# Turning x later and moving gate projections between groups in a hand-ordered state space stage

## The chip, the cores and the metric

One Trainium2 chip, one of its cores. The metric is the device time of one execution in microseconds (us), where less is better. Everything is float32 at the kernel's edges.

## What is computed

Two layers of a hybrid encoder on one sequence of 512 tokens and 1024 channels. In each layer one input projection feeds a state space branch (Mamba-2 style, forward and backward), a differential attention branch and a cross-attention branch; the branches are merged by gates computed from x. What matters here is the state space branch and the gates:

```python
proj = jnp.einsum('bsd,de->bse', x, w_in[layer])
z, xbc, dt_raw, dq, dk, dv, dg, cq, cg, gl = jnp.split(proj, splits, axis=-1)
# _ssd_branch: 32 heads of 64 channels, 4 groups of 8 heads, state 128, chunks of 128 tokens
xbc = jax.nn.silu(_centred_dwconv(xbc, conv_w, conv_b))      # 5 taps; x 2048, B 512, C 512 channels
y_diag = jnp.einsum('bcqgn,bcsgn,bgrcqs,bcsgrp->bcqgrp', cm, bm, decay, xs)
states = jnp.einsum('bcqgn,bgrcq,bcqgrp->bcgrpn', bm, decay_states, xs)
# scan over the 4 chunks: h -> h * chunk_decay + states; prev = the h before each chunk
y_off  = jnp.einsum('bcqgn,bcgrpn,bgrcq->bcqgrp', cm, prev, jnp.exp(a_cum))
y = (y_fwd + y_bwd + d_skip * xs) * jax.nn.silu(z);  y = _rmsnorm(y, norm_w)
...
merged = gates[:, :, 0] * (y_ssd @ w_br_ssd) + gates[:, :, 1] * (y_diff @ w_br_diff) + gates[:, :, 2] * (y_cross @ w_br_cross)
```

## The kernel before

Channels lie on the partitions and the 512 tokens along the free axis. A float32 matrix product is made from three matmuls on a high and a low part (`xh`, `xl` of the input; `wh`, `wl` of a weight; `mm3`). The work is a list of **units**. A unit is 128x1024 floats of weights (`wr`, 512 KB, loaded by SP at line 134), which ACT rounds to `wh` (line 87) and DVE subtracts to `wl` (line 77), and then 24 matmuls of 128x512 on TensorE (PE, line 99) into one bank of PSUM (`pj`, three buffers). A unit can be cut in the middle, and other matmuls put there.

The state space stage `ssd()` takes the four groups one after another in each layer. For a group g the units are: `bu` and `cu` (B and C), `xu(g, 0..3)` (x, 128 channels each, block b), `zu(g, 0..3)` (the gate z) and, for the group before, `wu(p, 0..3)` with p = g-1 (that branch's output projection: 24 matmuls for each of its two 128-channel outputs over half of a unit, copied or added into `mrg`). Twelve units are **early gates** (`gu`): gate projections that are not needed here and fill the stage; each ends in a Tanh on ACT (`tg`) and a store by SP. Between units stand small pieces of PE work:

- `bturn`, `xturn(g, b)`: four 128x128 transposes of the convolved, SiLU'd B or x block (`bC`, `xsC`) into the bank `pt` (one buffer); ACT copies it to `bT` or to a quarter of `xsT`. The convolution of an x unit is one scaled copy on ACT and four taps on DVE (`acc`, line 80), then SiLU on ACT.
- `states(g, 0..2)`: DVE multiplies `xsT` by the decays to `xw` (two buffers), and PE forms two state matrices of the chunk; ACT or DVE turns them into `prev`.
- `expos(g, b)`, no PE work: for each of the block's two heads SP loads a row of cumulative sums, broadcast to 128 partitions, into `ab` (two buffers, 512 KB, line 551); DVE takes the minimum with a mask, ACT makes eight exponentials of 128x128 in place, DVE adds the two directions and multiplies by `gs` into `m` (three buffers). The next load into the same `ab` buffer can be issued when that `m` is done.
- `block(g, b)`: 6 matmuls with `prev`, 16 with `m` (22 of 128x128 in all, more rows in the trace), then on DVE and ACT the output `y`, split into `yh` and `yl` for `wu`.

ACT needs another function table for the exponentials than for SiLU and Tanh: an `ACT_TABLE_LOAD` stands at each change between them.

**What sets the order.** PE's order in this stage is written out by hand: `U(unit, pieces...)` places a unit with pieces in its middle, `J(piece)` a piece between units, and the stage runs under `self.tc.manual_schedule(engines={mybir.EngineType.PE})`. The orders of ACT, DVE and SP are made by the Tile scheduler when the kernel is built. Each engine works its own list off in order.

Of the kernel before, what the change touches and what calls it, by code (L numbers as in the profile page):

```python
# [51 lines left out]
class Net:  # L52
# [391 lines left out]
    def ssd(self, l):  # L444
# [54 lines left out]
        def xpart(g, b):  # L499
            def f(wh, wl):  # L500
                x = yield from self.proj2(wh, wl)
                xc = B["xsC", g, b] = self.t(self.sp, [P, S], f"xsC{b}")
                self.conv(x, 4 * g + b, xc)
            return f
# [28 lines left out]
        def zpart(g, b):  # L533
            def f(wh, wl):
                ps = yield from self.proj2(wh, wl)
                sz = B["sz", g, b] = self.t(self.sp, [P, S], "sz", bufs=2)
                self.act(sz, ps, AF.Silu)
            return f
# [57 lines left out]
        def wpart(g, u):  # L596
            def f(wh, wl):
                yh, yl = G["y", g]
                pss = [self.bank(self.pj, "pj") for _ in range(2)]

                ks = ((0, 1, 2), (3,)) if u == 0 else ((0, 1, 2, 3),)
                for n, kk in enumerate(ks):
                    for i, ps in enumerate(pss):
                        for k in kk:
                            c = slice(k * 256 + i * P, k * 256 + (i + 1) * P)
                            self.mm(ps, wl[:, c], yh[:, k, :], k == 0, False)
                            self.mm(ps, wh[:, c], yh[:, k, :], False, False)
                            self.mm(ps, wh[:, c], yl[:, k, :], False, k == 3)
                        if 3 in kk:
                            o = self.br[:, 2 * u + i, :]  # L610
                            if g == 0:
                                self.act(o, ps)
                            else:
                                self.tt(o, o, ps, ALU.add)
                        if n == i == 0:
                            yield
            return f
# [63 lines left out]
        def U(unit, *amid):  # L681
            gen, u = unit

            def f(wh, wl):
                g = gen(wh, wl)
                next(g, None)
                for fn, *args in amid:
                    fn(*args)
                next(g, None)
            self.T(f, u)  # L690

        def J(fn, *args):
            self.T(lambda: fn(*args))

        def bu(g):
            return bpart(g), (l, UB + g)

        def cu(g):
            return cpart(g), (l, UC + g)

        def xu(g, b):
            return xpart(g, b), (l, UXS + 4 * g + b)

        def zu(g, b):
            return zpart(g, b), (l, UZ + 4 * g + b)

        def wu(g, u):
            return wpart(g, u), (l, UBS + 4 * g + u)

        def gu():  # L710
            return early.pop(0)
# [36 lines left out]
        for g in range(1, 4):  # L748
            p = g - 1
            U(bu(g))  # L750
            if g == 1:
                J(states, 0, 2)
                U(zu(p, 1), (block, p, 0))
            else:
                J(block, p, 0)
                U(zu(p, 1))
            J(expos, p, 1)
            U(cu(g))
            U(gu())
            J(block, p, 1)  # L760
            U(xu(g, 0), (bturn, g))
            J(expos, p, 2)
            U(zu(p, 2), (within, g))
            U(xu(g, 1))
            J(block, p, 2)
            J(xturn, g, 0)
            U(zu(p, 3))
            J(expos, p, 3)
            U(xu(g, 2))
            J(xturn, g, 1)  # L770
            J(block, p, 3)
            U(xu(g, 3))
            U(gu(), (xturn, g, 2))
            U(wu(p, 0))
            J(xturn, g, 3)
            U(wu(p, 1))
            U(wu(p, 2), (states, g, 0))
            J(states, g, 1)
            U(wu(p, 3))
            J(states, g, 2)  # L780
            J(expos, g, 0)
            U(zu(g, 0))
# [648 lines left out]
```

## Time and profile before

| what | value |
|---|---|
| device time, median of 3 runs | 2189.69 us (2188.62 to 2190.12) |
| the profiled execution: its time | 2190.09 us |
| the profiled execution: its span | 2188.3 us |
| PE busy | 2148.1 us, 98% |
| DVE busy, ACT busy | 71%, 53% |
| mean granted TensorE clock | 0.997 of full |
| state space stage of layer 0, of layer 1 | about 80 to 500 us, about 1150 to 1640 us |

The span is the time from the first to the last instruction in the profiled execution; the 1.8 us around it belong to the execution's own time. Busy times are sums over the span. A row of the timeline has the start in us, the duration, engine, line, operation and tiles, and, where the engine stood idle just before, in brackets the idle time and what ended it.

### The profile page before, as it was taken

Reading aid. Unit: us, or ns where it says so; the run is one execution under the profiler, and the core shown is the slowest. Engines: PE = TensorE matmul, PEld = TensorE weight load, DVE = VectorE, ACT = ScalarE, POOL = GpSimd, SP = SyncE. Lnnn points to the kernel's source line nnn. Section 1 sums busy time; section 2 is a strip of 40 time slices with the busy share of each in tenths; the row PEclk is TensorE's granted clock in tenths of the full one; section 3 lists DMA queues with packets and bytes.
Section 4 is the critical chain, followed back from the end, with each engine's and each line's share of the span. In section 5 each row is a group of like instructions: output and inputs, shape, how many; then the busy total and the mean of one; then the engine's idle time right before and its main releaser. Section 6 shows DMA issues by size and latency. Waiting matters only on the chain.

```text
span 2188.3 us, 29240 instructions
## 1 busy us (share of the span) xinstructions
PE 2148.1 (98%) x11122; PEld 1787.3 (82%) x11122; DVE 1546.6 (71%) x2404; ACT 1152.1 (53%) x2035; POOL 61.3 (3%) x38
## 2 busy tenths in 40 slices
PE   8999999999999999999999999999999999999998
PEld 6787878788888888887888777878788888888876
DVE  5677777869554788766566677878675547888667
ACT  5676757554432455543345676858533325555430
POOL 0010101010000000000000000101000000000000
PEclk9999999999999999999999999999999999999999
DMA  4654545454554433324564654545444334333253
GB/s 162 159 148 136 163 122 169 121 144 149 173 168 123 137 113 107 112 83 153 153 208 128 164 148 135 165 134 160 127 135 135 106 113 130 112 111 107 91 160 111
DMA packets 111984, 299.46 MB, mean 137 GB/s; under 512 B 12716, under 2 KB 13284, under 8 KB 111588
## 3 DMA queue, kind: packets, MB, share of 16 engines
q1 hardware_dynamic: 111844, 297.60, 46.0%
q8 instruction: 87, 1.43, 0.3%
q14 instruction: 53, 0.43, 0.1%
HBM read 257.16 MB, written 19.43 MB: 126 GB/s over the span
## 4 chain that ended last, share of the span: by engine, by line
PE 78%; DVE 9%; DMA 7%; ACT 2%; issue 2%; SPq 0%; DVEq 0%; ACTq 0%
PE pj L99 61%; PE pm L99 14%; DMA ab<-dab 4%; PE pt L107 2%; DVE acc L80 2%; DVE wl L77 2%; DMA wr<-wu 2%; DVE y L77 1%; DMA fth<-rd 1%; DVE eb L77 1%; ACT wh L87 1%; DVE ab L77 1%; ACT L87 1%; DVE y L80 1%; DMA mkv<-dkv 0%
## 5 line engine op out<-in xcount | busy, mean ns | idle before, releaser
L99 PE MATMUL pj<-xh,wl 128*128 128x512 f32 x1664 | 668.3, 402 | 0.2 <-DVE wl L77 0.2
L99 PE MATMUL pj<-xh,wh 128*128 128x512 f32 x1664 | 652.5, 393 | 8.1 <-ACT xh L87 6.0
L99 PE MATMUL pj<-xl,wh 128*128 128x512 f32 x1664 | 652.0, 392 | 0.0
L77 DVE TENSOR_TENSOR wl<-wr,wh 128x1024 fp32r<-128x1024 f32 x330 | 403.6, 1224 | 154.8 <-ACT wh L87 154.2
L87 ACT ACTIVATE wh<-wr 128x1024 fp32r<-128x1024 f32 x330 | 347.5, 1054 | 248.4 <-PE pj L99 169.5
L99 PEld LDWEIGHTS pj<-xh,wh 128*128 128x128 f32 x1664 | 314.0, 189 | 76.1 <-ACT xh L87 6.0
L99 PEld LDWEIGHTS pj<-xh,wl 128*128 128x128 f32 x1664 | 314.0, 189 | 70.8 <-issue 6.7
L99 PEld LDWEIGHTS pj<-xl,wh 128*128 128x128 f32 x1664 | 314.5, 189 | 65.0 <-issue 2.9
L87 ACT ACT_TABLE_LOAD x107 | 137.3, 1283 | 93.4 <-DVE ab L77 31.7
L87 ACT ACTIVATE ab<-ab,bias 128x128 f32<-128x128 f32 x512 | 161.3, 390 | 14.6 <-DVE ab L77 13.8
L80 DVE SCALAR_TENSOR_TENSOR acc<-pj,pr,acc 128x510 f32<-128x510 f32 (+1 forms) x192 | 142.2, 744 | 32.6 <-ACT acc L87 31.7
L77 DVE TENSOR_TENSOR ab<-ab,cst 128x1024 f32<-128x1024 f32 x64 | 78.2, 1223 | 72.9 <-DMA ab<-dab 72.8
L1059 DVE TENSOR_REDUCE fmx<-pm 128x1 f32<-128x512 f32 x128 | 85.0, 685 | 46.8 <-PE pm L99 46.8
L99 PE MATMUL pj<-yh,wl 128*128 128x512 f32 x256 | 106.1, 415 | 0.5 <-DVE mrg L77 0.5
L87 ACT ACTIVATE fpp<-pm,fmx 128x512 f32<-128x512 f32 x128 | 87.1, 685 | 33.8 <-DVE fmx L1059 33.8
L99 PE MATMUL pj<-dy,wh 128*128 128x512 f32 (+1 forms) x384 | 102.6, 356 | 0.9 <-DVE dy L77 0.9
L99 PE MATMUL pj<-yl,wh 128*128 128x512 f32 x256 | 100.2, 391 | 0.1
L99 PE MATMUL pj<-yh,wh 128*128 128x512 f32 x256 | 99.8, 390 | 0.0
L77 POOL TENSOR_TENSOR sqa<-sqa,sz 128x512 f32<-128x512 f32 x32 | 60.1, 1878 | 887.6 <-ACT sz L87 887.6
L99 PE MATMUL pj<-cy,wh 128*128 128x512 f32 x256 | 78.8, 389 | 0.0
L99 PEld LDWEIGHTS pj<-dy,wh 128*128 128x128 f32 x384 | 67.5, 188 | 13.2 <-DVE dy L77 2.1
L99 PE MATMUL pj<-wh,xl 128*128 128x256 f32 x256 | 73.3, 286 | 0.0
(274 smaller groups left out, 3309.2 us busy)
## 6 DMA issues: line engine op xcount, KB each, us to landing
wr<-wu SPq DMA_DIRECT2D x336, 512.0 KB, 3.7
ab<-dab SPq DMA_DIRECT2D x64, 512.0 KB, 5.6
eb<-deb SPq DMA_DIRECT2D x64, 256.0 KB, 5.9
mkv<-dkv SPq DMA_DIRECT2D x16, 512.0 KB, 4.1
rsw<-rx SPq DMA_DIRECT2D x64, 128.0 KB, 2.3
dy<-dy SPq DMA_DIRECT2D x32, 256.0 KB, 2.3
dgt<-tg SPq DMA_DIRECT2D x24, 256.0 KB, 3.9
dkv<-mo SPq DMA_DIRECT2D x16, 256.0 KB, 4.4
```

The lines of the kernel that those rows point to most:

```text
L77: (eng or self.nc.vector).tensor_tensor(out=out, in0=a, in1=b, op=op)
L80: self.nc.vector.scalar_tensor_tensor(out=out, in0=a, scalar=s, in1=b, op0=op0, op1=op1)
L87: self.nc.scalar.activation(out=out, in_=a, func=f, **kw)
L99: self.nc.tensor.matmul(out=out, lhsT=a, rhs=b, start=first, stop=last)
L107: self.nc.tensor.transpose(out=out, in_=x, identity=self.ident)
L1059: nc.vector.tensor_reduce(out=mx[:, c:c + 1], in_=ps, axis=AX.X, op=ALU.min)
```

## The change

In the loop over groups 1 to 3, for both layers. The four turns of x are placed later: turn 0 after `zu(p, 3)` instead of before it, turn 1 from ahead of `block(p, 3)` to the middle of `xu(g, 3)`, turn 2 from the middle of the gate behind `xu(g, 3)` to its end, turn 3 from ahead of `wu(p, 1)` to its middle. The early gates, two in each of these groups before, become three, two and one: in group 1 one is added ahead of `xu(1, 2)`, and in group 3 the one behind `cu(3)` is left out, where `block(2, 1)` goes into the middle of `xu(3, 0)`, ahead of `bturn`.

```diff
             U(cu(g))
-            U(gu())
-            J(block, p, 1)
-            U(xu(g, 0), (bturn, g))
+            if g < 3:
+                U(gu())
+                J(block, p, 1)
+            U(xu(g, 0), *(((block, p, 1),) if g == 3 else ()), (bturn, g))
             J(expos, p, 2)
             U(zu(p, 2), (within, g))
             U(xu(g, 1))
             J(block, p, 2)
+            U(zu(p, 3))
             J(xturn, g, 0)
-            U(zu(p, 3))
             J(expos, p, 3)
+            if g == 1:
+                U(gu())
             U(xu(g, 2))
-            J(xturn, g, 1)
             J(block, p, 3)
-            U(xu(g, 3))
-            U(gu(), (xturn, g, 2))
+            U(xu(g, 3), (xturn, g, 1))
+            U(gu())
+            J(xturn, g, 2)
             U(wu(p, 0))
-            J(xturn, g, 3)
-            U(wu(p, 1))
+            U(wu(p, 1), (xturn, g, 3))
             U(wu(p, 2), (states, g, 0))
```

The instructions of PE, DVE, SP and POOL are as many as before; ACT has 1867 rows instead of 1875, since four table loads a layer are gone.

The scheduler's orders change with it. On DVE, in group 1 of layer 0, where the third x block is convolved (`acc_231` before, `acc_237` now). `ab_290` before and `ab_296` and `ab_298` now are the loads of `expos(1, 0)`. Before:

```order
L77 TENSOR_TENSOR wl_228_1310<-wr_226_1307,wh_227_1309 128x1024
L77 TENSOR_TENSOR ab_290_1644<-ab_290_1644,cst_4_81 128x1024
L80 SCALAR_TENSOR_TENSOR acc_231_1339<-pj_229_1313,pr_18_127,acc_231_1339 128x510
L77 TENSOR_TENSOR eb_221_1276<-pm_233_1352,eb_221_1276 128x384
L80 SCALAR_TENSOR_TENSOR acc_231_1339<-pj_229_1313,pr_18_127,acc_231_1339 128x511
L77 TENSOR_TENSOR eb_221_1276<-pm_234_1353,eb_221_1276 128x384
L80 SCALAR_TENSOR_TENSOR acc_231_1339<-pj_229_1313,pr_18_127,acc_231_1339 128x511
L80 SCALAR_TENSOR_TENSOR y_236_1371<-xsC3_92_576,pr_18_127,pm_235_1360 128x512
L80 SCALAR_TENSOR_TENSOR acc_231_1339<-pj_229_1313,pr_18_127,acc_231_1339 128x510
```

and of the changed kernel:

```order
L77 TENSOR_TENSOR wl_228_1310<-wr_226_1307,wh_227_1309 128x1024
L77 TENSOR_TENSOR ab_296_1679<-ab_296_1679,cst_4_81 128x1024
L77 TENSOR_TENSOR wl_234_1345<-wr_232_1342,wh_233_1344 128x1024
L77 TENSOR_TENSOR ab_298_1694<-ab_298_1694,cst_4_81 128x1024
L77 TENSOR_TENSOR eb_221_1276<-pm_238_1381,eb_221_1276 128x384
L80 SCALAR_TENSOR_TENSOR acc_237_1374<-pj_235_1348,pr_18_127,acc_237_1374 128x510
L77 TENSOR_TENSOR eb_221_1276<-pm_239_1382,eb_221_1276 128x384
L80 SCALAR_TENSOR_TENSOR acc_237_1374<-pj_235_1348,pr_18_127,acc_237_1374 128x511
L80 SCALAR_TENSOR_TENSOR y_241_1400<-xsC3_92_576,pr_18_127,pm_240_1389 128x512
L80 SCALAR_TENSOR_TENSOR acc_237_1374<-pj_235_1348,pr_18_127,acc_237_1374 128x511
L77 TENSOR_TENSOR y_241_1400<-y_241_1400,eb_221_1276 128x384
L80 SCALAR_TENSOR_TENSOR acc_237_1374<-pj_235_1348,pr_18_127,acc_237_1374 128x510
```

The minimum of the second head (`ab_298`; before it was `ab_292`, twelve rows behind the last of these taps) now also stands ahead of the taps.

On ACT, at `wu(0, 0)` and `wu(0, 1)` of the same group (`pj_253`/`pj_254` before and `pj_259`/`pj_260` now are the two halves of `wu(0, 0)`; `pt_255` before is turn 3, `pt_266` now). Before:

```order
L87 ACTIVATE ab_292_1659<-ab_292_1659,bias_87_541 128x128
L87 ACT_TABLE_LOAD
L87 ACTIVATE xsC3_241_1411<-acc_242_1412 128x512
L87 ACTIVATE mrg_20_131<-pj_253_1466 128x512
L87 ACTIVATE mrg_20_131<-pj_254_1467 128x512
L87 ACTIVATE xsT_174_989<-pt_255_1494 128x4x128
L87 ACTIVATE wh_257_1502<-wr_256_1500 128x1024
L87 ACT_TABLE_LOAD
L87 ACTIVATE ab_292_1659<-ab_292_1659,bias_87_541 128x128
L87 ACTIVATE mrg_20_131<-pj_259_1506 128x512
L87 ACTIVATE ab_292_1659<-ab_292_1659,bias_87_541 128x128 x6
```

and of the changed kernel:

```order
L87 ACTIVATE xsC3_247_1446<-acc_248_1447 128x512
L87 ACT_TABLE_LOAD
L87 ACTIVATE ab_323_1845<-ab_323_1845,bias_87_541 128x128 x4
L87 ACTIVATE mrg_20_131<-pj_259_1501 128x512
L87 ACTIVATE ab_323_1845<-ab_323_1845,bias_87_541 128x128
L87 ACTIVATE mrg_20_131<-pj_260_1502 128x512
L87 ACTIVATE wh_262_1531<-wr_261_1529 128x1024
L87 ACTIVATE ab_323_1845<-ab_323_1845,bias_87_541 128x128 x3
L87 ACTIVATE ab_325_1860<-ab_325_1860,bias_87_541 128x128
L87 ACTIVATE mrg_20_131<-pj_264_1535 128x512
L87 ACTIVATE xsT_174_989<-pt_266_1550 128x4x128
```

The copies of `wu(0, 0)` into `mrg` stood ahead of the exponentials; now four exponentials of `ab_323`, a load of `expos(1, 1)`, stand ahead of the first and one more ahead of the second.

On DVE, at the states of group 1 (`xw_266` and `xw_269` before, `xw_272` to `xw_281` now). Before:

```order
L77 TENSOR_TENSOR ab_292_1659<-ab_292_1659,cst_4_81 128x1024
L80 SCALAR_TENSOR_TENSOR acc_242_1412<-pj_240_1386,pr_18_127,acc_242_1412 128x510
L77 TENSOR_TENSOR wl_252_1463<-wr_250_1460,wh_251_1462 128x1024
L77 TENSOR_TENSOR ab_317_1810<-ab_317_1810,cst_4_81 128x1024
L77 TENSOR_TENSOR xw_266_1555<-xsT_174_989,wst_46_297 128x512
L77 TENSOR_TENSOR xw_269_1561<-xsT_174_989,wst_46_297 128x512
L77 TENSOR_TENSOR wl_258_1503<-wr_256_1500,wh_257_1502 128x1024
L77 TENSOR_TENSOR ab_292_1659<-ab_292_1659 128x512
```

and of the changed kernel:

```order
L77 TENSOR_TENSOR ab_323_1845<-ab_323_1845,cst_4_81 128x1024
L77 TENSOR_TENSOR wl_258_1498<-wr_256_1495,wh_257_1497 128x1024
L77 TENSOR_TENSOR ab_325_1860<-ab_325_1860,cst_4_81 128x1024
L77 TENSOR_TENSOR wl_263_1532<-wr_261_1529,wh_262_1531 128x1024
L77 TENSOR_TENSOR ab_323_1845<-ab_323_1845 128x512
L77 TENSOR_TENSOR m_324_1857<-ab_323_1845,gs_203_1154 128x512
L77 TENSOR_TENSOR xw_272_1590<-xsT_174_989,wst_46_297 128x512
L77 TENSOR_TENSOR xw_275_1596<-xsT_174_989,wst_46_297 128x512
L77 TENSOR_TENSOR ab_325_1860<-ab_325_1860 128x512
L77 TENSOR_TENSOR wl_269_1572<-wr_267_1569,wh_268_1571 128x1024
L77 TENSOR_TENSOR ab_353_2025<-ab_353_2025,cst_4_81 128x1024
L77 TENSOR_TENSOR xw_278_1615<-xsT_174_989,wst_46_297 128x512
```

The first two `xw` stood behind the minimum of one load (`ab_317`); now the minima of two loads stand ahead of them, and `xw_278`, the third, stands behind the minimum of a third load (`ab_353`), whose buffer comes free with `m_324` five rows above it.

## Rows read from the trace of the kernel before

**Rows 1.** The page's first part: busy time, share of the span and instructions of each engine.

```profile
PE 2148.1 (98%) x11122; PEld 1787.3 (82%) x11122; DVE 1546.6 (71%) x2404; ACT 1152.1 (53%) x2035; POOL 61.3 (3%) x38
```

**Rows 2.** The waits of PE over the whole execution: what waited for what, us in total, times, the longest. Three of its rows.

```profile
PE pt L107 <- ACT xsC L87: 9.4, 7, 3.8
...
PE pm L99 <- DVE m L77: 1.6, 2, 1.0
...
PE pj L99 <- DVE mrg L77: 0.5, 1, 0.5
```

**Rows 3.** Timeline of PE, layer 0. In group 1: the start of `block(0, 2)`, turn 0, the first matmul of `zu(0, 3)`, of `xu(1, 2)`, then turn 1, the `m` part of `block(0, 3)`, turn 2, the gate's second half and `wu(0, 0)`. Last, in group 2, turn 2 and the matmul behind it.

```profile
144.49 1.50 PE L99 MATMUL pm<-cC,prev 128*128 128x128 f32 x12
...
146.95 0.66 PE L107 MATMUL pt<-cst,xsC 128*128 128x128 f32 x4
147.36 0.47 PE L99 MATMUL pj<-xh,wl 128*128 128x512 f32 x1
...
152.93 0.39 PE L99 MATMUL pj<-xh,wl 128*128 128x512 f32 x1
...
158.37 0.60 PE L107 MATMUL pt<-cst,xsC 128*128 128x128 f32 x4
...
160.90 1.09 PE L99 MATMUL pm<-m,xsT 128*64 128x128 f32 x16 [0.59 <-DVE m L77]
...
174.21 0.66 PE L107 MATMUL pt<-cst,xsC 128*128 128x128 f32 x4 [3.83 <-ACT xsC L87]
174.62 0.47 PE L99 MATMUL pj<-xh,wl 128*128 128x512 f32 x1
...
179.04 0.40 PE L99 MATMUL pj<-yh,wl 128*128 128x512 f32 x1
...
281.96 0.60 PE L107 MATMUL pt<-cst,xsC 128*128 128x128 f32 x4
282.32 0.48 PE L99 MATMUL pj<-xh,wl 128*128 128x512 f32 x1
```

**Rows 4.** Timeline of PE, layer 1, group 1: its three waits (turn 1, `block(0, 3)`, turn 2).

```profile
1295.62 0.55 PE L107 MATMUL pt<-cst,xsC 128*128 128x128 f32 x3 [0.68 <-ACT xsC L87]
...
1298.64 0.55 PE L99 MATMUL pm<-m,xsT 128*64 128x128 f32 x6 [1.03 <-DVE m L77]
...
1310.91 0.66 PE L107 MATMUL pt<-cst,xsC 128*128 128x128 f32 x4 [2.78 <-ACT xsC L87]
```

**Rows 5.** The stretches behind the two longest waits: start and end, length, busy time and count of PE, PEld, DVE, ACT and POOL, then the granted clock (1.00 is full), the DMA share and GB/s.

```profile
174.30:177.70 3.40, 3.40 (x13) 2.79 (x14) 3.40 (x5) 3.08 (x5) 0.66 (x1) 0.67 0.76 225
...
1311.00:1314.40 3.40, 3.40 (x13) 2.80 (x14) 3.40 (x5) 3.09 (x5) 0.66 (x1) 0.66 0.76 225
```

**Rows 6.** Timelines of SP, DVE and ACT, layer 0, ahead of turn 2: the issue of a load of `ab` on SP; on DVE the minimum of that load and the first tap of x block 2; on ACT the table load and SiLU of x block 1, its scaled copy for x block 2 and the copy of turn 1, then the two table loads and what stands between them and behind.

```profile
160.30 0.38 SPq L551 DMA_DIRECT2D ab<-dab  x1
```

```profile
166.71 1.23 DVE L77 TENSOR_TENSOR ab<-ab,cst 128x1024 f32<-128x1024 f32 x1 [4.73 <-DMA ab<-dab]
167.85 0.74 DVE L80 SCALAR_TENSOR_TENSOR acc<-pj,pr,acc 128x510 f32<-128x510 f32 x1
```

```profile
157.31 0.64 ACT L87 ACTIVATE xsC<-acc 128x512 f32<-128x512 f32 x1
...
161.07 0.59 ACT L87 ACTIVATE xsT<-pt 128x512 f32<-128x512 f32 x1
...
168.00 1.28 ACT L87 ACT_TABLE_LOAD   x1 [4.77 <-DVE ab L77]
169.29 2.45 ACT L87 ACTIVATE ab<-ab,bias 128x128 f32<-128x128 f32 x8
172.23 1.28 ACT L87 ACT_TABLE_LOAD   x1 [0.48 <-DVE acc L80]
173.52 0.63 ACT L87 ACTIVATE xsC<-acc 128x512 f32<-128x512 f32 x1
```

**Rows 7.** Two more loads of `ab` in the same group: issue on SP, and the minimum on DVE that waited for the landing.

```profile
180.19 0.38 SPq L551 DMA_DIRECT2D ab<-dab  x1
...
199.97 0.38 SPq L551 DMA_DIRECT2D ab<-dab  x1
```

```profile
186.23 1.23 DVE L77 TENSOR_TENSOR ab<-ab,cst 128x1024 f32<-128x1024 f32 x1 [2.49 <-DMA ab<-dab]
...
205.52 1.22 DVE L77 TENSOR_TENSOR ab<-ab,cst 128x1024 f32<-128x1024 f32 x1 [0.28 <-DMA ab<-dab]
```

**Rows 8.** What ACT and DVE did for `wu(0, 0)` and the first states of group 1: the copies into `mrg`, and the first two `xw`.

```profile
184.52 1.06 ACT L87 ACTIVATE mrg<-pj 128x512 f32<-128x512 f32 x2
```

```profile
187.37 1.29 DVE L77 TENSOR_TENSOR xw<-xsT,wst 128x512 f32<-128x512 f32 x2
```

**Rows 9.** From the page's lists of groups (busy us, mean ns of one, idle time before) and of DMA issues (count, size, median us from issue to landing).

```profile
L87 ACT ACT_TABLE_LOAD x107 | 137.3, 1283 | 93.4 <-DVE ab L77 31.7
L87 ACT ACTIVATE ab<-ab,bias 128x128 f32<-128x128 f32 x512 | 161.3, 390 | 14.6 <-DVE ab L77 13.8
...
ab<-dab SPq DMA_DIRECT2D x64, 512.0 KB, 5.6
```

**Rows 10.** Layer 0, group 3: on DVE the second `m` of `block(2, 2)`, on PE the part of that block that reads it.

```profile
357.81 0.68 DVE L77 TENSOR_TENSOR m<-ab,gs 128x512 f32<-128x512 f32 x1
```

```profile
365.49 1.09 PE L99 MATMUL pm<-m,xsT 128*64 128x128 f32 x16
```

## The prediction

> **What bounds the kernel now.** I read the page's busy shares first: PE works 98% of the span [rows 1]. With PE's instructions unchanged in number, the change can only alter what PE waits for, at which clock it runs, and what a transpose costs at its new place. So the waits of PE came next, then its timeline around each of them, then the clock, and last what DVE, ACT and SP do ahead of the longest wait.
>
> Of the list of waits the change touches three rows, 11.5 us together: the turns of x waiting for SiLU (9.4 us in 7 waits), `block` waiting for `m` (1.6 in 2), and a `wu` unit waiting for `mrg` (0.5) [rows 2]. In layer 0, group 1, PE stands 0.59 us before the `m` part of `block(0, 3)` and 3.83 before turn 2 [rows 3]; layer 1 has 0.68, 1.03 and 2.78 at the same places [rows 4]. That is 8.91 of the 11.5; groups 2 and 3 hold the other 2.6.
>
> The two longest waits also cost clock. Behind them the granted clock is 0.67 and 0.66, a mean over a stretch of which most is at half speed, 1.2 instead of 2.4 GHz [rows 5]. The half unit behind the wait takes from 174.62 to 179.04, 4.42 us, where a whole unit takes 152.93 - 147.36 = 5.57 [rows 3], so half of one 2.79: 1.6 us lost. Layer 1 shows the same length at the same mean clock, so another 1.6. No such loss follows the waits of about 1 us.
>
> Why turn 2 waits: DVE stands idle for 4.73 us for a load of `ab`, issued at 160.30 and landed by 166.71; that minimum stands ahead of the taps of x block 2 on DVE, and the eight exponentials behind it stand on ACT ahead of the table load (172.23) and SiLU (173.52) for which PE waits [rows 6]. Turn 2 could have gone at about 170.4, half a unit into the gate.
>
> **What the change removes.** Turn 2 is asked for later in group 1. From 146.95, where nothing has changed, PE now has: `zu(0, 3)` 5.57 us, turn 0 alone 282.32 - 281.96 = 0.36, the added gate 5.57, `xu(1, 2)` 5.44 (158.37 - 152.93), `block(0, 3)` 2.46 (146.95 - 144.49), `xu(1, 3)` with turn 1 inside about 6.1, the gate 5.44 [rows 3]. The sum puts turn 2 at 177.9. `block(0, 3)` now stands a whole gate later than its `m`, so that its waits go; turn 1 gets as much. I count as removed all of 8.91 and 3.2 of clock in group 1, and 2.6 in groups 2 and 3, where turns come half a unit to a unit later against waits of up to about 1 us: 14.7 us in all.
>
> **What takes its place in group 1.** The minimum of `ab` still leads, and a second load's minimum now stands ahead of the taps too. From ACT's order: after the table load (ending 169.3) seven exponentials at about 0.3 us each (2.45 for eight [rows 6]) to 171.4, then the scaled copy 0.65. The taps on DVE, with what is mixed in, took from 167.85 to 172.2 [rows 6], 4.4 us; begun at 172.05 they end at 176.4, load and SiLU take 1.28 and 0.63, and turn 2 is possible at 178.4: **0.6 us** of wait.
>
> Next is `wu(0, 0)`, whose second bank of PSUM was the gate's and is free only after the gate's Tanh. Tanh now stands behind that SiLU, `yh`, `sz`, a scaled copy and a weight rounding; the same row of work went from 157.31 to 161.07, 3.8 us with one `sz` more [rows 6], so Tanh ends near 182. PE asks at 178.4 + 0.4 + 9 matmuls of 0.23 = 180.9: **1.1 us**.
>
> Then `wu(0, 1)`. Its second bank needs the copy of `wu(0, 0)` into `mrg`. That copy stood ahead of any new load at 184.52 [rows 8]; now it follows four exponentials of `ab_323`. That buffer comes free when DVE is through `m_297`, behind taps (176.4), two `y` steps, a weight part, two sums and `yl`, 4.1 us and 0.65 of its own: 181.2. The landing takes 5.6 us by the median [rows 9]: 186.8. Minimum 1.2, four exponentials 1.2 and the copy 0.6 end at 189.9. PE is there at 178.8 + 5.6 + 1.1 + 2.8 + 0.4 = 188.7: **1.2 us**.
>
> Last, the second states. `xw_278` stands on DVE behind the minimum of `ab_353`, whose load waits for `m_324`, and that for the last exponentials of `ab_323`: 189.9 plus four more exponentials, a copy and a weight rounding (2.8), sum and product (1.3) give 194.0; landed at 199.6, minimum and `xw` done at 201.4. PE stands there at 188.7 + 1.2 + 2.8 + 2.8 + 1.3 + 2.8 = 199.6; the second `xw` of the pair comes later than its matmul by about 0.3: **2 us**. At this place the first two `xw` were done at 188.7 before [rows 8], far ahead.
>
> These make 4.9 us a layer, 9.8 for both. All of them are new: before, the copies and `xw` stood ahead of the loads.
>
> **The bounds of this term.** Three loads in this group show issue to minimum 6.4, 6.0 and 5.6 us [rows 6, 7], and the median of all is 5.6 [rows 9]. I take 5.6, since the copies of `wr` that share the queue are as many as there. At 6.4 each of the two landings adds 0.8 a layer, 3.2 us in all. Below, the waits can't be less than those that depend on no landing, 0.6 and 1.1, 3.4 for both layers.
>
> The Trainium skill, DMA: Bandwidth & Descriptors, "Anatomy of one DMA", gives about 2.0 us plus bytes over 436 thousand per us, which for 512 KB would be 3.2 us, an estimate from that page for a load issued by GpSimd. The trace disagrees for these loads, 5.6 [rows 9]; by the page the last two waits would be gone.
>
> **What else it costs.** A turn that stands alone between units costs 0.36 us and the unit behind it 5.57 instead of 5.44, together 0.08 more than the 0.41 of one beside a `block` [rows 3]. Twelve turns a kernel or so lose such a neighbour and as many gain a middle; **1.0 us** at most. In groups 2 and 3 the loads are issued far enough ahead for the turns; the second `xw` of a pair comes just late, **0.5 us** in all. The gate taken from group 3 leaves its cover 5.4 us shorter there: the second `m` of `block(2, 2)` is done at 358.5 and read at 365.5 [rows 10], so that 1.6 us are left and I cost it at nothing; with that cover gone too it would be a wait like the 0.6 to 1.0 of `block(0, 3)`, twice. Four table loads fewer a layer free 8 x 1.283 = 10.3 us of ACT [rows 9], which is not what PE waits for except in the chains above, where it is counted.
>
> The Trainium skill, ScalarE: Activation LUTs, "What ACT_TABLE_LOAD costs", puts a switch at 2.66 us, 1.38 of it a drain, and speaks against the change, since turn 2's chain holds a switch: by it 1.4 us a layer more. The trace doesn't bear it out: the load at 168.00 lasts 1.28 and exponentials start at 169.29 [rows 6].
>
> **The sum.** -14.7 + 9.8 + 0.5 + 1.0 = -3.4. The profiled execution took 2190.09, which gives 2186.7; its time is 0.4 over the median of the runs, so **2186.3** for the median. A measurement of this kernel can tell about 0.2%, 4.4 us, from no change: 2185.3 and 2194.1 are the borders.
>
> **The rivals.**
> - *The landings stop mattering* (0.12). If `ab_323` and `ab_353` land about 2 us sooner than 5.6, as they would if `wr` loads were out of their way, the last two waits a layer vanish: 6.4 less, 2180. Against it: no load here was under 5.6. The Trainium skill, DMA: Bandwidth & Descriptors, by its sum above, would have it so.
> - *Nothing new at all* (0.08). The scheduler's list costs no wait, as when Tanh and SiLU come earlier than I set them: -14.7 + 1.5, 2176.5.
> - *Waits only move* (0.12). Each wait of before comes back at its new place; the sum is 0 to 1 us over before, 2190.
> - *Slower: the chain of `ab` loads gets the clock too* (0.13). Each load is issued when the `m` two loads before is done, so lateness is handed on. At 6.4 us a landing, three links a layer (the next is for the third states) add 2.4 us each layer, 4.8, and a wait of more than the 2.78 that was followed by half clock in layer 1 [rows 4, 5] brings 1.6 a layer: 2186.3 + 4.8 + 3.2 = 2194.3. It decides where the wait before the second states, 2 us by my sum, passes about 2.8. For it: the load ahead of turn 2 took 6.4. Against: that load stood beside two `eb` loads.
> - *My forecast* (0.55), with its own range 2182.5 to 2191; about 0.2 of it lies under 2185.3, the rest within 0.2%.
>
> **How the numbers follow.** Faster by over 0.2%: 0.12 + 0.08 + 0.20 = 0.40. Slower: the last rival, 0.13. Within: 0.12 + 0.35 = 0.47. The range from 2179 to 2195 leaves out the case of no new waits, and little beyond the slow one.
>
> **What would show it.** The list of PE's waits should lose most of the 9.4 us for `xsC` and gain rows of `pj` waiting for ACT's `tg` and `mrg`, and of `pm` waiting for DVE's `xw`, of 1 to 2 us, at 181, 188 and 200 us and at the same places in layer 1. There should be no half clock in either layer. DVE should stand idle for `ab` ahead of `xw_278`. If the mean granted clock stays below 1 at these places, or group 2 or 3 shows new waits over 1 us, steps of mine are wrong; if the landings take 4 us or 7, the size is.

## The result

The changed kernel takes 2196.3 us (median of 12 runs, 2190.4 to 2199.8) against 2190.1 for the kernel before: ratio 1.0028, 95% interval 1.0018 to 1.0038. Timed again beside two experiments it took 2192.4, ratio 1.0014 (1.0004 to 1.0024). Three executions of 2920 to 4343 us, against 2170 to 2204 for all others, are left out of the medians here and below. So it is slower by 0.28% in the first series and by 0.14% in the second, where I had forecast 2186.3 with a chance of 0.13 for slower; the range of 2179 to 2195 just misses the first of the two medians.

The profiled execution of the changed kernel has a span of 2195.1 us, 6.8 over that of before. PE's waits in it, those that bear on the change:

```profile
PE pj L99 <- ACT yh L87: 6.8, 2, 3.7
...
PE pt L107 <- ACT xsC L87: 2.3, 2, 1.2
...
PE pj L99 <- ACT tg L87: 1.9, 2, 0.9
PE pm L99 <- DVE xw L77: 1.7, 2, 0.9
...
PE pj L99 <- ACT mrg L87: 1.5, 2, 1.1
```

The 9.4 us for `xsC` of [rows 2] are down to 2.3, and the 1.6 for `m` are gone. The rows for `tg`, `xw` and `mrg` are the new waits of group 1 that the prediction had. The first row is not in it: the two longest waits of the stage, for `yh`. PE's timeline says where each stands (layer 0, and last the row of layer 1 for `yh`):

```profile
177.08 0.66 PE L107 MATMUL pt<-cst,xsC 128*128 128x128 f32 x4 [1.16 <-ACT xsC L87]
180.75 0.50 PE L99 MATMUL pj<-yh,wl 128*128 128x512 f32 x1 [0.95 <-ACT tg L87]
184.66 0.50 PE L99 MATMUL pj<-yh,wl 128*128 128x512 f32 x1 [0.22 <-DVE acc L80]
189.18 0.50 PE L99 MATMUL pj<-yh,wl 128*128 128x512 f32 x1 [1.05 <-ACT mrg L87]
...
200.23 2.33 PE L99 MATMUL pm<-xw,bT 128*128 128x512 f32 x4 [0.83 <-DVE xw L77]
...
477.33 0.50 PE L99 MATMUL pj<-yh,wl 128*128 128x512 f32 x1 [3.06 <-ACT yh L87]
...
1618.53 0.50 PE L99 MATMUL pj<-yh,wl 128*128 128x512 f32 x1 [3.70 <-ACT yh L87]
```

477 us and 1618 us are the end of the stage: `wu(3, 0)`, whose last quarter needs `yh` of `block(3, 3)`. The kernel before has no wait there. Behind both waits the clock is at half for 6.8 us; in layer 1 (columns as in [rows 5]):

```profile
1618.90:1622.30 3.40, 3.40 (x12) 2.60 (x11) 1.74 (x3) 0.97 (x2) 1.28 (x1) 0.50 0.35 141
1622.30:1625.70 3.40, 3.40 (x10) 2.82 (x11) 2.10 (x8) 0.18 (x1) 0.00 (x0) 0.50 0.04 10
```

6.8 us at half speed lose 3.4. The end of the stage thus costs 3.06 + 3.70 + 2 x 3.4 = 13.6 us. Group 1 costs 4.2 us in layer 0 (the first five rows) and 3.6 in layer 1. With the 14.7 us of old waits and half clock gone, that makes -14.7 + 7.8 + 13.6 = +6.7.

That the spans differ by 6.8 is partly chance. From the first transposes of the cumulative sums (`pt<-cst,cum`) to the last matmul on `yh`, the stage of layer 0 takes 426.1 us instead of 422.1, and that of layer 1 takes 427.2 instead of 422.3: 8.9 us more. Outside of them this execution is 2.1 us quicker than that of the kernel before, 2.0 of it before the first of these transposes, where nothing was changed. So 2.2 us of what the stages lost are in none of the rows above.

**Why `yh` is late.** ACT of the changed kernel at the end of layer 0's stage (`xsT<-pj,hgb` is the Tanh of a gate here):

```profile
457.91 1.28 ACT L87 ACT_TABLE_LOAD   x1 [2.39 <-DVE ab L77]
459.20 0.99 ACT L87 ACTIVATE ab<-ab,bias 128x128 f32<-128x128 f32 x3
460.10 0.67 ACT L87 ACTIVATE xsT<-pj,hgb 128x512 f32<-128x512 f32 x1
460.67 1.05 ACT L87 ACTIVATE wh<-wr 128x1024 fp32r<-128x1024 f32 x1
461.62 1.56 ACT L87 ACTIVATE ab<-ab,bias 128x128 f32<-128x128 f32 x5
...
466.53 0.72 ACT L87 ACTIVATE yh<-y,pr 128x512 fp32r<-128x512 f32 x1 [3.35 <-DVE y L77]
...
469.58 1.05 ACT L87 ACTIVATE wh<-wr 128x1024 fp32r<-128x1024 f32 x1
...
476.56 0.72 ACT L87 ACTIVATE yh<-y,pr 128x512 fp32r<-128x512 f32 x1 [4.39 <-DVE y L77]
```

and DVE:

```profile
456.61 1.23 DVE L77 TENSOR_TENSOR ab<-ab,cst 128x1024 f32<-128x1024 f32 x1 [3.69 <-DMA ab<-dab]
...
461.75 1.23 DVE L77 TENSOR_TENSOR wl<-wr,wh 128x1024 fp32r<-128x1024 f32 x1 [1.84 <-ACT wh L87]
462.89 0.74 DVE L80 SCALAR_TENSOR_TENSOR y<-xsC,pr,pm 128x512 f32<-128x512 f32 x1
...
470.67 1.23 DVE L77 TENSOR_TENSOR wl<-wr,wh 128x1024 fp32r<-128x1024 f32 x1 [2.62 <-ACT wh L87]
471.81 1.01 DVE L77 TENSOR_TENSOR eb<-pm,eb 128x384 f32<-128x384 f32 x2
```

The starts of `block(3, 2)` and `block(3, 3)` on PE:

```profile
453.97 1.50 PE L99 MATMUL pm<-cC,prev 128*128 128x128 f32 x12
...
467.44 1.50 PE L99 MATMUL pm<-cC,prev 128*128 128x128 f32 x12
```

The same place in the kernel before, ACT, then DVE, then PE (`block(3, 3)`, and the first matmul that needs its `yh`):

```profile
458.44 0.69 ACT L87 ACTIVATE xsT<-pj,hgb 128x512 f32<-128x512 f32 x1 [0.35 <-PE pj L99]
459.02 1.04 ACT L87 ACTIVATE wh<-wr 128x1024 fp32r<-128x1024 f32 x1
461.94 1.28 ACT L87 ACT_TABLE_LOAD   x1 [1.87 <-DVE ab L77]
...
477.54 0.72 ACT L87 ACTIVATE yh<-y,pr 128x512 fp32r<-128x512 f32 x1 [4.00 <-DVE y L77]
```

```profile
472.58 0.56 DVE L77 TENSOR_TENSOR eb<-pm,eb 128x384 f32<-128x384 f32 x1 [0.67 <-PE pm L99]
```

```profile
471.71 1.50 PE L99 MATMUL pm<-cC,prev 128*128 128x128 f32 x12
...
478.38 0.44 PE L99 MATMUL pj<-yh,wl 128*128 128x512 f32 x1
```

Before, the Tanh of gate (0, 6) and the weight rounding behind it stood ahead of the last exponentials; they ran while ACT would have waited for the load of `ab`. In the changed kernel the scheduler put the table load and three exponentials ahead of them, and these wait for the landing. `wh` slips behind it, DVE's `wl` waits for `wh`, the output steps of `block(3, 2)` wait behind `wl`, and `yh` of `block(3, 3)` starts at 476.56, only 1 us ahead of the 477.54 of before, though PE is there 4 us sooner (2 of them by chance, from the start of the execution). Before, DVE stood idle for 0.67 us at this place until PE was through, so that `yh` followed the block itself: it was done at 478.26, 6.55 us behind the block's start at 471.71, and PE needed it at 478.38, 6.67 us behind that start. Those 0.1 us are the same in every kernel that doesn't wait for `yh`. The room for a late list was DVE's idle time, 0.67 us here and 0.83 in layer 1; in the changed kernel `yh` is done 9.84 us behind the start of its block.

The Tanh at 460.10 stands between two parts of the exponentials, and no `ACT_TABLE_LOAD` stands on either side of it. So in this trace a Tanh runs among exponentials without a change of table, unlike what the section on the kernel before says; the table loads here stand between exponentials and SiLU.

### The profile page after: what moved, and what is told of

Its sections match the earlier page's. It is cut to its first block, busy times and chain, and to the rows that moved or that the text cites. A ratio compares the mean times of both kernels' runs of the same rounds, so it can differ in the third digit from the quotient of the medians.

```text
span 2195.1 us, 29245 instructions
## 1 busy us (share of the span) xinstructions
PE 2152.3 (98%) x11122; PEld 1788.5 (81%) x11122; DVE 1545.9 (70%) x2404; ACT 1140.5 (52%) x2027; POOL 61.0 (3%) x38
## 4 chain that ended last, share of the span: by engine, by line
PE 77%; DVE 9%; DMA 9%; ACT 3%; issue 2%; SPq 0%; DVEq 0%; ACTq 0%
PE pj L99 60%; PE pm L99 14%; DMA ab<-dab 6%; PE pt L107 2%; DVE wl L77 1%; DVE ab L77 1%; DMA wr<-wu 1%; DVE acc L80 1%; DVE y L77 1%; ACT wh L87 1%; ACT ab L87 1%; ACT L87 1%; DVE m L77 1%; DMA fth<-rd 1%; DVE prev L77 1%
## 5 line engine op out<-in xcount | busy, mean ns | idle before, releaser
L77 POOL TENSOR_TENSOR sqa<-sqa,sz 128x512 f32<-128x512 f32 x32 | 59.7, 1867 | 889.2 <-ACT sz L87 889.2
```

The source lines that it names most:

```text
L77: (eng or self.nc.vector).tensor_tensor(out=out, in0=a, in1=b, op=op)
```

## Experiments: one part of the change at a time

Two theories on the wait for `yh`. A: one gate less in group 3 lets PE run ahead of what DVE and ACT can do there. B: the new list at the end of the stage makes `yh` late. Each ratio is to the kernel before on the same chip: 2188.2 us for the turns alone, the gates alone, the third gate from group 2 and the later norm; 2187.9 for the second series of the turns, the other gate, and three buffers on the changed kernel and on the turns; 2189.0 for the gate in group 0, the Tanh and the changed kernel again; 2187.6 for three buffers on the kernel before. The ratios on record differ from the quotients of these medians by up to 0.0005.

**The turns alone.**

```diff
+            U(zu(p, 3))
             J(xturn, g, 0)
-            U(zu(p, 3))
...
-            J(xturn, g, 1)
             J(block, p, 3)
-            U(xu(g, 3))
-            U(gu(), (xturn, g, 2))
+            U(xu(g, 3), (xturn, g, 1))
+            U(gu())
+            J(xturn, g, 2)
```

(and turn 3 inside `wu(p, 1)`; gates stay two a group.)

> The four turns moved as in the change, the early gates two a group and block(2, 1) where they were. Theory A (the gate missing from group 3 lets PE reach wu(3, 0) before yh of block(3, 3) can be done): no wait for yh at the end of the stage, no half clock there, and most of the 14.7 us of old waits gone, against new waits of at most 4 us a layer in group 1: 2178 to 2186 us. Theory B (the turns' new places, by way of the order that the scheduler gives DVE and ACT, make yh late): the wait of 3 to 4 us for yh and 6.8 us at half clock show here too, 2190 to 2198 us.

2176.9 us, ratio 0.9948 (0.9932 to 0.9965). The time is 1 us under A's range and far from B's. A second series, for its timeline:

> The turns alone once more, for its timeline: 2177 to 2179 us as timed before. Theories A and B both expect no wait for yh at the end of the stage and no half clock; the waits in group 1 should be under 3 us a layer.

2176.6 us, ratio 0.9946 (0.9930 to 0.9962). No wait for `xsC`, `yh`, `tg`, `mrg` or `xw` is left, no half clock in the stage, and of the waits in question there are only

```profile
PE pm L99 <- DVE m L77: 2.3, 2, 1.3
```

So the turns give back 11.2 and 11.4 us by themselves, as 14.7 less the waits for `m` that stay here (2.3) and about 1 us for their places would. B as it was first set, that the turns' places bring the late list, falls. What is left of B is that the gates bring it; in that form it expects no wait here, as A does.

**The gates alone,** the turns where they were.

```diff
-            U(gu())
-            J(block, p, 1)
-            U(xu(g, 0), (bturn, g))
+            if g < 3:
+                U(gu())
+                J(block, p, 1)
+            U(xu(g, 0), *(((block, p, 1),) if g == 3 else ()), (bturn, g))
...
             J(expos, p, 3)
+            if g == 1:
+                U(gu())
             U(xu(g, 2))
```

> The early gates three, two, one and block(2, 1) inside xu(3, 0) as in the change, the turns where they were. DVE's order at the end of the stage is that of the kernel before. Theory A: wu(3, 0) waits 2 to 4 us for yh and the clock is halved behind it, 5 to 7 us a layer; with the wait of group 1 eased by the added gate 2192 to 2203 us. Theory B: no wait for yh, 2180 to 2190 us.

2198.0 us, ratio 1.0047 (1.0029 to 1.0064). Two rows of its waits:

```profile
PE pt L107 <- ACT xsC L87: 13.0, 8, 3.7
PE pm L99 <- DVE xw L77: 6.3, 2, 3.4
```

There is no wait for `yh`, as B had it, but the time is A's: without the later turns the added gate makes group 1 worse than before, by 3.4 and 2.9 us at the states, and groups 2 and 3 wait for turns again. PE lost its lead in these waits, so that this run doesn't refute A.

**The third gate from group 2 instead of group 3**, all else as in the change.

```diff
-            if g < 3:
+            if g != 2:
                 U(gu())
                 J(block, p, 1)
-            U(xu(g, 0), *(((block, p, 1),) if g == 3 else ()), (bturn, g))
+            U(xu(g, 0), *(((block, p, 1),) if g == 2 else ()), (bturn, g))
```

> The changed kernel with the third gate of group 1 taken from group 2 instead of group 3 (block(1, 1) inside xu(2, 0), block(2, 1) back behind its gate). DVE's order at the end of the stage is that of the kernel before. Theory A: no wait for yh at the end of the stage, since group 3 has its two gates; 7 to 14 us under the changed kernel unless group 2 waits instead (by 2 us a layer at most): 2182 to 2190 us. A rival, that the lost cover is needed wherever it is taken: the lead lost in group 2 is never regained and yh waits as before, 2193 to 2199 us.

2184.0 us, ratio 0.9979 (0.9970 to 0.9989). No wait for `yh`, no half clock; the group 1 waits are as in the changed kernel:

```profile
PE pm L99 <- DVE xw L77: 2.4, 2, 1.3
...
PE pj L99 <- ACT mrg L87: 1.9, 2, 1.6
PE pj L99 <- ACT tg L87: 1.9, 2, 0.9
```

A gate can be spared in group 2, and not at this place in group 3. Against the turns alone on the same chip (2176.9) this kernel is 7.0 us worse. The two differ by the gate added to group 1 and the one taken from group 2. By the waits it is 5.7: 8.0 us of new ones in group 1, less the 2.3 for `m` that they replace.

**The gate put into group 0 instead of group 1;** group 3 has one, as in the change.

```diff
         J(expos, 0, 0)
         U(gu())
+        U(gu())
         J(states, 0, 0)
...
-            if g == 1:
-                U(gu())
             U(xu(g, 2))
```

> The turns as in the change, the gates two, two, one, and the gate that the change adds to group 1 put at the end of group 0 instead. ACT's list at the end of the stage is that of the changed kernel. The waits of group 1 for tg, mrg and xw, 4 us a layer in the changed kernel, should be gone if the added gate makes them; the wait for yh with its half clock, 2 to 7 us a layer, should stay by both theories A and B: 2184 to 2192 us. If the gate's place in group 1 were not the cause, 2193 to 2199 us.

2184.2 us, ratio 0.9979 (0.9969 to 0.9988; single runs 2178 to 2188). On this chip the changed kernel took 2192.4, 8.2 more. The waits for `tg` and `mrg` are gone, and of those for `xw` one of 0.7 us is left, in group 0. Those for `yh` stay, at 1.80 and 1.65 us, less than I had set and without half clock in the profiled execution, which at 2178.5 is the fastest of the ten:

```profile
PE pj L99 <- ACT yh L87: 3.4, 2, 1.8
...
PE pm L99 <- DVE m L77: 2.4, 2, 1.4
```

So the two edits to the gates cost separately: the one in group 1 in that group, the one missing in group 3 at the end.

## Experiments: lead or list

**The other gate of group 3 left out,** on the changed kernel.

```diff
-            if g < 3:
-                U(gu())
-                J(block, p, 1)
-            U(xu(g, 0), *(((block, p, 1),) if g == 3 else ()), (bturn, g))
+            U(gu())
+            J(block, p, 1)
+            U(xu(g, 0), (bturn, g))
...
             U(xu(g, 3), (xturn, g, 1))
-            U(gu())
+            if g < 3:
+                U(gu())
             J(xturn, g, 2)
```

> The changed kernel, but group 3 gives up the gate behind xu(3, 3) instead of the one behind cu(3), and block(2, 1) stands between units as before. Group 3 has one gate, as in the change, while DVE's order at the end of the stage is that of the kernel before (the weight part ahead of the minimum of ab, the output steps of block(3, 2) ahead of the last sum and product). Theory A (one gate less in group 3 lets PE get there before yh can be done): wu(3, 0) waits 2 to 4 us for yh in both layers, with half clock behind it, 2190 to 2199 us. Theory B (the scheduler's new list at the end of the stage makes yh late): no wait for yh, 2180 to 2187 us.

2188.9 us, ratio 1.0001 (0.9991 to 1.0010), between the two ranges. No wait for `yh`; DVE stands waiting for PE at the output of `block(3, 3)`:

```profile
471.29 1.23 DVE L77 TENSOR_TENSOR eb<-pm,eb 128x384 f32<-128x384 f32 x2 [1.03 <-PE pm L99]
```

This looks like B, and isn't enough for it. Turn 2, now asked for early in group 3, waits 1.44 us in each layer, and PE has no lead left: `block(3, 1)` starts 9.45 us ahead of its `yl` (443.48 and 452.93), against 9.97 in the kernel before and 11.68 in the changed one (440.49 and 452.17).

**The Tanh ahead of the exponentials, and nothing else.** The changed kernel, where the last head's exponentials read their biases through a copy that needs the Tanh of gate (0, 6):

```diff
...
+                bz = self.bias
+                if g == 3 and b == 3 and hh == 1:
+                    bz = self.t(sp, [P, 4, 64], "bz")
+                    src = self.bias[:, :, h:h + 33:32]
+                    self.stt(bz[:, :, h:h + 33:32], gt[3 + b][:, 0:8].rearrange("p (c d) -> p c d", d=2), 0.0, src, ALU.mult, ALU.add)
...
-                        self.act(ab[:, d, c, :], ab[:, d, c, :], AF.Exp, bias=self.bias[:, c, j:j + 1])
+                        self.act(ab[:, d, c, :], ab[:, d, c, :], AF.Exp, bias=bz[:, c, j:j + 1])
```

> The changed kernel with one operation of 128x8 more on DVE in each layer: the biases of the last head's exponentials are read through a copy that needs the Tanh of gate (0, 6), zero times its value added. This puts that Tanh and the weight rounding behind it ahead of the exponentials in ACT's list, as in the kernel before; gates and turns stay as in the change. Theory A (the lead alone): wu(3, 0) waits 2 to 4 us for yh, and half clock stays, 2191 to 2198 us. Theory B (the list alone): no wait, 2180 to 2184 us. Both in part: PE is 1.7 us further ahead of the yl before it than in the kernel before, whose DVE had 0.7 us to spare, so a wait of about 1 us without half clock, 2182 to 2187 us.

2185.0 us, ratio 0.9981 (0.9972 to 0.9991), where the changed kernel took 2192.4 on the same chip. ACT at the end of the stage:

```profile
456.12 0.68 ACT L87 ACTIVATE xsT<-pj,hgb 128x512 f32<-128x512 f32 x1
456.69 1.06 ACT L87 ACTIVATE wh<-wr 128x1024 fp32r<-128x1024 f32 x1
457.77 1.28 ACT L87 ACT_TABLE_LOAD   x1
...
473.64 0.72 ACT L87 ACTIVATE yh<-y,pr 128x512 fp32r<-128x512 f32 x1 [4.00 <-DVE y L77]
```

PE doesn't wait for `yh` and its clock stays full, with the gates, turns and lead of the changed kernel (`block(3, 1)` starts 12.0 us ahead of its `yl`, in the changed kernel 11.7). Of the three cases set out it is the list alone by the waits, with a time 1 us above the one that I gave for it, inside the range of the third case.

One difference is left: the last load of `ab` lands 0.9 us sooner here, measured against PE. The traces of all the kernels tell what that is worth. For each, two times were read off: how long behind the start of `block(3, 2)` DVE begins the last minimum of `ab`, and how long behind the start of `block(3, 3)` `yh` is done, which PE needs at 6.7 us.

| list at the end of the stage | kernels, both layers of each | minimum, us | `yh` done, us |
|---|---|---|---|
| of the kernel before | before, turns alone, gates alone, gate from group 2, other gate | 0.9 to 2.4 | 6.6 in all ten |
| with the Tanh first | this one | 1.7, 1.7 | 6.6, 6.6 |
| of the changed kernel | changed (two profiles), gate in group 0, later norm | 1.2 to 3.3 | 8.4 to 10.5 |

In the last row the two columns differ by 7.2 us in all eight cases: each microsecond of a later landing is one of a later `yh`. A landing like the 1.7 of this kernel would still cost about 2 us there; the later norm, at 1.7 in layer 1, waited 2.08. With the list of before, a later minimum only shortens DVE's idle time ahead of the output of `block(3, 3)`; the two add up to 3.1 us wherever the idle time is under its most, 1.97. So the landings of the changed kernel's first profile, 2.6 and 3.3, would have cost nothing and at most 0.2 us with that list, an estimate from these rows. The list with the Tanh first has less room, 0.13 and 0.20 us of idle time, so that its own zero is in part due to the sooner landing: at 2.6 it would wait for about 0.7 us. So the missing gate acts through the scheduler's list, and how much it costs hangs on the landing; PE's lead by itself costs next to nothing.

**The changed kernel again,** beside these.

> The changed kernel once more, beside the other two: 2192 to 2199 us, a wait for yh of 1.5 to 4 us in each layer, and half clock of 3.4 or 6.8 us behind each that is over about 2 us.

2192.4 us. The waits for `yh` and the stretches behind them:

```profile
477.02 0.79 PE L99 MATMUL pj<-yh,wl 128*128 128x512 f32 x1 [2.98 <-ACT yh L87]
...
1614.30 0.50 PE L99 MATMUL pj<-yh,wl 128*128 128x512 f32 x1 [2.44 <-ACT yh L87]
```

```profile
476.80:480.10 3.30, 3.08 (x9) 2.40 (x9) 1.56 (x3) 0.81 (x3) 1.28 (x1) 0.50 0.54 210
480.20:483.50 3.30, 3.30 (x18) 2.84 (x19) 2.57 (x9) 0.84 (x1) 0.00 (x0) 1.00 0.01 2
1614.30:1617.70 3.40, 3.35 (x16) 2.34 (x17) 2.42 (x7) 1.52 (x2) 1.30 (x1) 1.00 0.45 183
```

3.4 us at half clock in layer 0 and none in layer 1, instead of 6.8 twice. This execution took 2190.0 and the first one 2196.8, which is 6.8 us: the waits for `yh` are 1.3 us shorter, and 13.6 - 3.4 = 10.2 us less at half clock give back 5.1. The spread of this kernel's runs goes the same way: of the first twelve, the fastest, 2190.4, had a mean granted clock of 0.999, and the four slowest, 2198.8 to 2199.8, had 0.994 to 0.995.

**The norm's small matmuls a unit later,** on the changed kernel.

```diff
         U(wu(3, 0))
-        J(norm)
         U(wu(3, 1))
+        J(norm)
         U(wu(3, 2))
```

> The changed kernel with the sum of squares' matmuls (eight of 128x1, the piece norm) a unit later, behind wu(3, 1). If these matmuls keep the clock at half for the second 3.4 us behind the wait for yh, the half clock is 3.4 instead of 6.8 us in each layer, and the time 3 us under the changed kernel. If the wait alone decides, 6.8 us at half clock stay, and so does the time, within 1 us, unless the later norm makes norm_spread late.

2193.1 us, ratio 1.0019 (1.0009 to 1.0028). In the profiled execution the waits for `yh` are 1.70 and 2.08 us, with no half clock behind the first and 3.4 us behind the second. The waits were shorter than in the changed kernel's profile, and the changed kernel with the norm in its place had 3.4 us and none in its second profile. The run doesn't tell the two apart; what makes it 6.8 us stays open.

## Experiments: the landing

**Three buffers for `ab`,** on the changed kernel.

```diff
-                ab = self.t(sp, [P, 2, 4, P], "ab", bufs=2)
+                ab = self.t(sp, [P, 2, 4, P], "ab", bufs=3)
```

> The changed kernel with three buffers for ab instead of two, so that a load can be issued one head earlier. If the late landings of ab are what makes both lists late (group 1: Tanh, mrg, xw; end of the stage: yh), the waits of 1 us in group 1 and that for yh go, and the half clock with it: 2175 to 2183 us. If PE's lead alone makes the wait for yh, it stays at 2 to 4 us with its half clock: 2186 to 2193 us.

2174.4 us, ratio 0.9933 (0.9916 to 0.9951). The idle time of DVE ahead of the minimum, in the changed kernel:

```profile
L77 DVE TENSOR_TENSOR ab<-ab,cst 128x1024 f32<-128x1024 f32 x64 | 78.2, 1222 | 64.1 <-DMA ab<-dab 64.1
```

and with three buffers:

```profile
L77 DVE TENSOR_TENSOR ab<-ab,cst 128x1024 f32<-128x1024 f32 x64 | 77.7, 1219 | 39.2 <-DMA ab<-dab 39.1
```

All of the waits for `yh`, `tg`, `mrg` and `xsC` are gone, though gates and turns are those of the change, and the time is 0.6 us under the range that I gave. The last minimum of `ab` now begins 13 to 14 us ahead of `block(3, 2)` instead of 2.6 and 3.3 behind it. The list there is another one too: no minimum and no exponentials of `ab` stand at this place any more. So the run shows that an earlier issue takes the waits away, not what the changed kernel's own list would cost with it.

**The same on the turns alone, and on the kernel before.**

> The turns alone, gates two a group, with three buffers for ab. If landings of ab cause what waits are left in groups 1 to 3, 1 to 3 us a layer go: 2172 to 2177 us. If they are hidden already it stays within 1.5 us of the turns alone, 2176 to 2179 us.

2172.0 us, ratio 0.9924 (0.9908 to 0.9939): 4.6 us under the turns alone, and the fastest median of all.

> The kernel before with three buffers for ab and nothing else. If the wait of turn 2 in group 1 is due to the landing of ab, as I read it ahead of the change, that wait (3.8 and 2.8 us) and its half clock (1.6 a layer) go, 9.8 us in all, and with them the waits for m: 2176 to 2181 us. If the turns' places are needed as well, waits for xsC of 1 to 4 us a layer stay and the time is 2181 to 2187 us.

2175.2 us, ratio 0.9941 (0.9924 to 0.9958), just under the first range: the waits for turn 2 in group 1 shrink to 0.66 and 0.25 us and their half clock is gone. The kernel before was bound at turn 2 by the landing of `ab`, as read; a buffer does as much against it as the turns do (12.4 us against 11.4), and both together give back 3.6 and 4.6 us more than either.

## Why the prediction was wrong

*What the change removes:* right. 9.4 us for `xsC` became 2.3, and `m` no longer waits; with the turns alone the gain is 11.4 us, and the `m` waits that stay there are those that the added gate takes away in the changed kernel.

*What takes its place in group 1:* right in every place, at 177, 181, 189 and 200 us, and too large in sum. Predicted were 0.6, 1.1, 1.2 and 2 us a layer. Measured in layer 0 were 1.16, 0.95, 1.05 and 0.83, in layer 1 1.09, 0.94, 0.45 and 0.89, with 0.22 more in each: 7.8 instead of 9.8. The wait before the second states was the most oversized. Its load was issued 0.5 us sooner than in my sum, and its minimum began 4.9 us behind the issue instead of 5.6:

```profile
193.49 0.38 SPq L551 DMA_DIRECT2D ab<-dab  x1
...
198.35 1.22 DVE L77 TENSOR_TENSOR ab<-ab,cst 128x1024 f32<-128x1024 f32 x1 [0.64 <-DMA ab<-dab]
```

That no load was under 5.6 us held only for the three that I had read: in the kernel before they take 4.7 to 8.3 us from issue to landing. The median of the changed kernel's page is 6.0, further still from the estimate of 3.2 worked out for a load issued by GpSimd from the Trainium skill, DMA: Bandwidth & Descriptors, "Anatomy of one DMA". The table load ahead of turn 2 starts at 175.10 in the changed kernel, and SiLU follows at 176.39. By the 2.66 us of the Trainium skill, ScalarE: Activation LUTs, "What ACT_TABLE_LOAD costs", it could not have come before 177.8; the trace disagrees here too.

*What else it costs:* the 0.5 us for `xw` in groups 2 and 3 did not come, and the 1.0 for the turns' places is shown by no row; 2.2 us of the stages' loss have no row at all.

*The gate taken from group 3:* this step failed. I wrote that "1.6 us are left and I cost it at nothing", from the `m` of `block(2, 2)` [rows 10]. That place is fine, but I followed the lost 5.4 us of cover no further. At the end of the stage the scheduler's list changes with the gate. I read the new lists in group 1 and not there, where the same exchange stands: exponentials that hang on a load ahead of a Tanh and a weight rounding. The term put at nothing costs 6.8 us of waits and 6.8 of clock in the first profile, and 7.4 us of the median in the run that undoes the exchange. That DVE had only 0.67 and 0.83 us of idle time to give there is shown by no list of PE's waits.

*The clock:* I expected no half clock after the change. The old ones are gone, as predicted, and new ones came at the end, up to twice as long as the old 3.4 us.

*The slower rival* had the time, 2194.3, by luck: its mechanism was a wait above 2.8 us at the second states with half clock behind it, and those waits were 0.83 and 0.89. What happened in another group shares with it that work behind the landing of `ab` comes late; lateness handed on from load to load is not shown.

## What to carry to other kernels

When work is taken out of a hand-written order, follow the lost cover to the end of the stage, and read the slack of every meeting there from the idle time of the engine that PE would wait for: where PE waited for nothing, DVE had 0.7 us left. Where other engines' lists are made by a scheduler, read the new lists at each place where a load's landing stands ahead of work that someone waits for; one dependency of 128x8 elements that put them back was worth 7.4 us. And a load that is issued one buffer earlier, with the lists that the scheduler then makes, took these waits away in three kernels: 2172 to 2175 us.

## What the runs showed of the hardware that I had not expected

Half clock behind a wait isn't a fixed price. Waits of PE of 3.06 and 3.70 us were followed by 6.8 us at half clock, where the 3.83 us of the kernel before were followed by 3.4; waits of 2.08 to 3.41 us by 3.4 in six cases, and those of 2.05, 2.13 and 2.44 us by none. Twice 3.4 us at half clock came behind shorter ones, ahead of layer 1's stage: at 1133.46 us in the changed kernel with three buffers and at 1150.43 in the kernel with the gates alone, each behind waits of 0.74 and 0.88. In the kernel with the gates alone it fell while PE still stood idle ahead of turn 2 (178.45 us, after 3.65 us of wait) and stayed for two stretches:

```profile
177.60:181.00 3.40, 2.55 (x8) 2.23 (x9) 3.40 (x7) 2.75 (x6) 0.00 (x0) 0.50 0.52 185
181.00:184.40 3.40, 3.40 (x9) 2.64 (x8) 3.40 (x4) 1.38 (x2) 1.65 (x1) 0.50 0.95 151
```

No norm matmuls stand there, so these aren't needed for 6.8 us. By these rows a wait of over 2 us should be priced with 0 to 3.4 us of lost clock, and not with one figure.
